# A recurrent state copied out of PSUM in the step that computes it, instead of one step later (gated linear attention inside a transformer block, one core)

## The chip, the cores and the metric

One core of a Trainium2 chip runs the whole block once. The metric is the device time of one execution in microseconds (us), the median of several runs. Engines are named as in the profile: PE is TensorE, DVE is VectorE, ACT is ScalarE, POOL is GpSimd, SP is SyncE (here a queue that issues DMAs).

## What is computed

One transformer block on 1024 tokens of width 1024: a modulated norm, one large input projection, sparse attention over the 256 best keys of each query beside gated linear attention (GLA), an output projection, and a gated feed-forward part. The part around the change is GLA's chunked recurrence:

```
def step(S, inp):
    ...
    o = (jnp.einsum('bhij,bhjv->bhiv', A, vc)
         + jnp.einsum('bhid,bhdv->bhiv', qc * jnp.exp(b), S))
    b_last = b[:, :, -1:, :]
    S = (jnp.exp(b_last)[:, :, 0, :, None] * S
         + jnp.einsum('bhjd,bhjv->bhdv', kc * jnp.exp(b_last - b), vc))
    return S, o
```

Each chunk's output needs the state S that the chunk before it left, and S is the old S, decayed, plus a product over the chunk's keys and values. The kernel uses chunks of 128 tokens (8 of them), and does two heads at a time: `gla0` is heads 0 and 1, `gla1` heads 2 and 3.

## The kernel before, in words

While PE works through the input projections (the *main* job list: groups of 24 or 48 matmuls called units here; lines L243 to L245 and L252 to L254), four *background* jobs advance beside it, a step at a time, at fixed rates per unit: `pump()` (L352) takes each generator in `bg` and calls `next` on it as often as its rate has come due. The four are `ta` and `td` (the search for the 256th largest score, one bit a round, `topk_act` L639 and `topk_dve` L611), and `gla0` and `gla1` (`gla_pair` L773). After each unit, `pin()` (L974) takes the PE and DVE instructions just traced and chains them with dependencies, so **PE and DVE run in exactly the order in which the program text produced them**. ACT, POOL and the DMA queues are not pinned; their order is set by the framework's scheduler.

A round of `ta` is three sign passes on ACT (L654, tiles of 1024, 896 and 768 columns, each with a count) and then four small DVE instructions (L656, L657, L659, L661), the last of which writes the thresholds `Ya` that the next round's passes read. A round of `td` follows on DVE: three counting passes (L625) and L629, L631. The two rounds stand one behind the other in DVE's order.

The end of `gla_pair` is the chunk loop (L882 to L904), nine steps for eight chunks. In step `ch` `chunk(ch)` puts these matmuls on PE, all into one PSUM tile `po` of the tag `pw`, of which there are two buffers: for each head L871 (within the chunk) and, from chunk 1 on, L874 (the carried state, which reads `St`), then L878 for both heads (what the chunk adds to the state). DVE reads that tile twice: L887 or L889 makes the new state `Sn` in SBUF (chunk 0: a copy; later `St` times `el` plus the product), and the pair of L899 adds the two heads' outputs into `gv`, after which ACT squares them (L902, two per chunk). A `pw` buffer is free for the chunk after next when its L899 pair is done.

In the version before, step `ch` begins with the state of chunk `ch - 1`, then issues `chunk(ch)`, then the L899 pair of chunk `ch - 1`:

```
                    Sn = small(P, tag="diag")
                    if ch == 1:
                        V.tensor_copy(Sn, po[:, P:2 * P])
...
            if ch < NT:
                po = chunk(ch)
```

Behind the chunk loop of `gla0` stand, on DVE, more rounds of the search, interleaved with the levels of `gla1`; ACT also casts weights (L219, `whi`) for the next projection there, into a ring of four buffers that PE frees.

Of the kernel before, what the change touches and what calls it, by code (L numbers as in the profile page):

```python
# [15 lines left out]
ALU = mybir.AluOpType  # L16

P = 128
L = 1024
D = 1024  # L20
NT = L // P
# [47 lines left out]
def hymba_block_kernel(  # L69
# [37 lines left out]
    def nm(s):  # L107
        uid[0] += 1
        return f"{s}_{uid[0]}"
# [7 lines left out]
    def ps(shape=(P, 512)):  # L117
        return psp.tile(list(shape), F32, tag="ps", bufs=4, name=nm("ps"))

    def pw(shape=(P, 1024)):  # L120
        return psp.tile(list(shape), F32, tag="pw", bufs=2, name=nm("pw"))

    def small(n=8, dt=F32, tag="sm", bufs=4):
        return sm.tile([P, n], dt, tag=tag, bufs=bufs, name=nm(tag))

    V, A, G, T, S = nc.vector, nc.scalar, nc.gpsimd, nc.tensor, nc.sync
# [261 lines left out]
    def gv_proj(p, w):  # L388
        drain("decay")
        gvt[p] = [g([P, 4, 256]) for _ in range(2)]  # L390
        if p == 0:
            bg["gla0"] = (gla_pair(0, gqk[0, 0], gqk[0, 1], gvt[0], bTs[0]), *RATE["gla0"])
        yield from proj_N_plain(w, gvt[p])
        if p == 0:
            bg["decay"] = (gla_decay(1), *RATE["decay"])
        else:
            drain("gla0")
            bg["gla1"] = (gla_pair(1, gqk[1, 0], gqk[1, 1], gvt[1], bTs[1]), *RATE["gla1"])
# [374 lines left out]
    def gla_pair(p, gq, gk, gv, bT):  # L773
# [48 lines left out]
        el = small(8, tag="el", bufs=2)  # L822
# [40 lines left out]
        St = None  # L863

        def chunk(ch):
            po = pw()
            gvc = gv[ch // 4][:, ch % 4, :]
            for h in range(2):
                hp, dv = slice(64 * h, 64 * h + 64), slice(h * P, (h + 1) * P)
                pd = po[:, h * 512:h * 512 + P]  # L870
                T.matmul(pd, lhsT=AT[ch // 4][:, (ch % 4) * 2 + h, :], rhs=gvc[:, dv],  # L871
                         start=True, stop=(ch == 0))
                if ch > 0:
                    T.matmul(pd, lhsT=gq[hp, ch * P:(ch + 1) * P], rhs=St[hp, :], start=False, stop=True)  # L874
            if ch < NT - 1:
                for h in range(2):
                    hp = slice(64 * h, 64 * h + 64)
                    T.matmul(po[hp, P:2 * P], lhsT=Kn[:, ch, hp], rhs=gvc[:, h * P:(h + 1) * P],  # L878
                             start=True, stop=True)
            return po  # L880

        for ch in range(NT + 1):  # L882
            if ch > 0:
                if ch < NT:
                    Sn = small(P, tag="diag")
                    if ch == 1:
                        V.tensor_copy(Sn, po[:, P:2 * P])  # L887
                    else:
                        V.scalar_tensor_tensor(Sn, St, el[:, ch - 1:ch], po[:, P:2 * P], ALU.mult, ALU.add)  # L889
                    St = Sn  # L890
                done = po
            if ch < NT:
                po = chunk(ch)
            if ch > 0:
                c0 = ch - 1
                gvc = gv[c0 // 4][:, c0 % 4, :]
                for h in range(2):
                    dv = slice(h * P, (h + 1) * P)
                    V.scalar_tensor_tensor(gvc[:, dv], gvc[:, dv], dg[:, 2 * c0 + h:2 * c0 + h + 1],  # L899
                                           done[:, h * 512:h * 512 + P], ALU.mult, ALU.add)  # L900
                    jk = small(P, BF16, tag="jk", bufs=2)
                    A.activation(jk, gvc[:, dv], AF.Square,  # L902
                                 accum_out=ssq_g[:, p, c0 * 2 + h:c0 * 2 + h + 1])
            yield  # L904
# [562 lines left out]
    for n in range(NDG):  # L1467
        ending = n == NDG - 1
        ahead = list(groups[n + 1]) if not ending else []
        for t in range(NT):  # L1470
# [5 lines left out]
            if t % 2:  # L1476
                po = [ps(), ps()]
            else:
                pq = pw()
                po = [pq[:, C0], pq[:, C1]]  # L1480
# [64 lines left out]
```

## Time and profile before

| | |
|---|---|
| three runs, us | 1398.03, 1402.06 (median), 1405.05 |
| the profiled execution, us | 1398.97 |
| its span, first to last instruction | 1397.2 |
| busy: PE, DVE, ACT, POOL | 1308.9, 906.9, 588.3, 413.8 us |
| mean granted TensorE clock | 0.982 of 2.4 GHz |
| chunk loop of gla0 / gla1 on PE | 248.3 to 293.6 us / 397.7 to 442.9 us |

Times inside the kernel are counted from the span's start. A timeline row gives start, duration, engine, line, operation, output and inputs, and in brackets how long the engine had been idle before it and which instruction ended that. Only the profiled execution has such rows; it was 3.09 us quicker than the median.

### The profile page before, as it was taken

What the parts mean: (1) busy time and instruction counts of PE and PEld (TensorE: products, weight loads), DVE (VectorE), ACT (ScalarE), POOL (GpSimd) and SP (SyncE); (2) the same over time, 40 slices, a digit from 0 to 9 for tenths busy, and PEclk for the clock granted to TensorE, in tenths of its full rate; (3) what the DMA queues carried; (4) which work ended last, traced back from release to release, by engine and by line L of the source; (5) the groups of instructions that cost most, each with busy time, mean ns of one, the idle gap of its engine ahead of it and who ended that gap; (6) DMA issues with size and microseconds to landing.
All of it is one profiled execution on the core that took longest, in us unless ns stands there. A gap on an engine that the chain in (4) does not pass through costs nothing.

```text
span 1397.2 us, 18382 instructions
## 1 busy us (share of the span) xinstructions
PE 1308.9 (94%) x6979; PEld 1095.5 (78%) x6979; DVE 906.9 (65%) x1539; ACT 588.3 (42%) x1078; POOL 413.8 (30%) x365
## 2 busy tenths in 40 slices
PE   5899999797799998899998999999999999999997
PEld 3777887696689877798876778878888878888886
DVE  3478899669987756783487666654454556576524
ACT  3367766666562235255673333333232335112202
POOL 3560122122400011213314434444344435222101
PEclk9999999899999999999999999999999999999999
DMA  9701001201120353740322233322222346254102
GB/s 264 216 15 31 16 16 46 76 16 47 60 61 16 121 165 107 271 139 28 121 76 76 91 119 108 121 91 76 91 76 87 125 151 211 95 164 148 46 15 106
DMA packets 93630, 136.36 MB, mean 98 GB/s; under 512 B 6403, under 2 KB 72038, under 8 KB 93542
## 3 DMA queue, kind: packets, MB, share of 16 engines
q1 hardware_dynamic: 89576, 121.49, 27.1%
q0 software_dynamic: 3808, 13.64, 3.1%
q8 instruction: 55, 0.90, 0.3%
q14 instruction: 33, 0.27, 0.1%
q10 hardware_dynamic: 158, 0.06, 0.0%
HBM read 111.04 MB, written 24.13 MB: 97 GB/s over the span
## 4 chain that ended last, share of the span: by engine, by line
PE 63%; DVE 18%; issue 5%; ACT 5%; DMA 3%; POOL 3%; SPq 2%; DVEq 0%; POOLq 0%; ACTq 0%
PE pw L1279 5%; PE pw L1280 4%; PE pw L1281 4%; PE ps L1279 4%; PE ps L1281 4%; PE ps L1280 4%; DVE junk_d L625 3%; PE ps L1486 3%; PE ps L1485 3%; PE ps L1487 3%; PE pw L1486 3%; PE pw L1487 3%; PE pw L1485 3%; ACT junk_a L654 2%; DVE h L798 2%
## 5 line engine op out<-in xcount | busy, mean ns | idle before, releaser
L654 ACT ACTIVATE junk_a<-g,Ya 128x1024 int8<-128x1024 f32 (+2 forms) x96 | 99.9, 1041 | 36.2 <-DVE Ya L661 30.4
L252 PE MATMUL ps<-whi,g 128*128 128x256 f32 x384 | 111.5, 290 | 0.0
L254 PE MATMUL ps<-wlo,g 128*128 128x256 f32 x384 | 109.2, 284 | 0.0
L253 PE MATMUL ps<-whi,g 128*128 128x256 f32 x384 | 109.1, 284 | 0.0
L1310 POOL TENSOR_TENSOR g<-g,h 128x512 f32<-128x512 f32 x33 | 52.2, 1582 | 139.4 <-issue 54.0
L1451 POOL TENSOR_TENSOR raw<-raw,g 128x1024 f32<-128x1024 f32 x22 | 58.2, 2649 | 111.2 <-DMA raw<-in_w_down_dram 101.7
L243 PE MATMUL ps<-g,whi 128*128 128x512 f32 x208 | 83.4, 401 | 0.5 <-DVE dg L853 0.5
L245 PE MATMUL ps<-g,wlo 128*128 128x512 f32 x208 | 81.5, 392 | 1.7 <-DVE wlo L220 1.7
L1281 PE MATMUL ps<-g,wlo 128*128 128x512 f32 x192 | 75.7, 394 | 6.3 <-DVE wlo L1272 6.2
L244 PE MATMUL ps<-g,whi 128*128 128x512 f32 x208 | 81.5, 392 | 0.0
L1279 PE MATMUL pw<-g,whi 128*128 128x512 f32 x192 | 76.9, 401 | 1.5 <-DVE h L1328 1.5
L1279 PE MATMUL ps<-g,wlo 128*128 128x512 f32 x192 | 75.8, 395 | 0.7 <-ACT g L1184 0.7
L252 PEld LDWEIGHTS ps<-whi,g 128*128 128x128 f32 x384 | 74.2, 193 | 2.7 <-issue 2.0
L1280 PE MATMUL ps<-g,wlo 128*128 128x512 f32 x192 | 75.4, 393 | 0.4 <-DVE g L1185 0.4
L1280 PE MATMUL pw<-g,whi 128*128 128x512 f32 x192 | 74.9, 390 | 0.0
L1281 PE MATMUL pw<-g,whi 128*128 128x512 f32 x192 | 74.8, 390 | 0.0
L253 PEld LDWEIGHTS ps<-whi,g 128*128 128x128 f32 x384 | 74.2, 193 | 0.0
L254 PEld LDWEIGHTS ps<-wlo,g 128*128 128x128 f32 x384 | 74.1, 193 | 0.1
L625 DVE TENSOR_SCALAR_CACHE_REDUCE junk_d<-g,Zd 128x640 bf16<-128x640 f32 (+5 forms) x96 | 71.4, 744 | 2.4
L1248 POOL TENSOR_TENSOR gs<-raw,raw 128x512 f32<-128x512 f32 x19 | 25.2, 1325 | 118.8 <-DMA raw<-in_w_gate_up_dram 94.0
L1272 DVE TENSOR_TENSOR whi<-gs,whi 128x512 fp32r<-128x512 f32 x44 | 39.1, 889 | 31.3 <-ACT whi L1271 30.8
L1272 DVE TENSOR_TENSOR wlo<-gs,wlo 128x512 fp32r<-128x512 f32 x44 | 39.1, 889 | 28.8 <-ACT wlo L1271 28.4
(408 smaller groups left out, 3823.0 us busy)
## 6 DMA issues: line engine op xcount, KB each, us to landing
raw<-in_w_gate_up_dram SPq DMA_DIRECT2D x42, 512.0 KB, 3.6
g<-in_w_mod_dram SPq DMA_DIRECT2D x24, 512.0 KB, 8.3
raw<-in_w_in_dram SPq DMA_DIRECT2D x24, 512.0 KB, 4.2
whi<-in_w_mod_dram POOLq DMA_DIRECT2D x24, 512.0 KB, 4.5
hid_d<-g SPq DMA_DIRECT2D x22, 512.0 KB, 3.0
raw<-in_w_down_dram SPq DMA_DIRECT2D x22, 512.0 KB, 4.4
gs<-hid_d SPq DMA_DIRECT2D x22, 512.0 KB, 3.4
g<-in_x_dram SPq DMA_DIRECT2D x16, 512.0 KB, 4.5
```

Source lines behind the costliest of these rows:

```text
L243: T.matmul(pt, lhsT=wh, rhs=rh, start=(k == 0), stop=False)
L252: T.matmul(pt, lhsT=rh, rhs=wh, start=(k == 0), stop=False)
L253: T.matmul(pt, lhsT=rl, rhs=wh, start=False, stop=False)
L254: T.matmul(pt, lhsT=rh, rhs=wl, start=False, stop=(k == KC - 1))
L625: V.tensor_scalar(junk_d[:, :W], top[t] if 0 < i < 16 else score[t], Z[:, j:j + 1].bitcast(F32), -float(TOPK), ALU.is_ge, ALU.add, accum_o ...
L654: A.activation(junk_a[:, :W], score[t], AF.Sign, bias=Y[:, j:j + 1].bitcast(F32), accum_out=acc[:, j:j + 1])
L1279: T.matmul(pt, lhsT=w[:, 0, kk, :], rhs=rh, start=(not more and kk == 0), stop=False, skip_group_check=more)
L1280: T.matmul(pt, lhsT=w[:, 0, kk, :], rhs=rl, start=False, stop=False, skip_group_check=more)
L1281: T.matmul(pt, lhsT=w[:, 1, kk, :], rhs=rh, start=False, stop=(kk == 3), skip_group_check=more)
L1485: T.matmul(po[m], lhsT=ah[:, r], rhs=wh[:, cc], start=(f == 0), stop=False)
L1486: T.matmul(po[m], lhsT=al[:, r], rhs=wh[:, cc], start=False, stop=False)
L1487: T.matmul(po[m], lhsT=ah[:, r], rhs=wl[:, cc], start=False, stop=(f == len(cur) - 1))
```

## The change

The new state of a chunk is made in the same step as the chunk's products, right behind them in the program text; the L899 pair of the chunk before follows it.

```diff
+        po = None
         for ch in range(NT + 1):
-            if ch > 0:
-                if ch < NT:
-                    Sn = small(P, tag="diag")
-                    if ch == 1:
-                        V.tensor_copy(Sn, po[:, P:2 * P])
-                    else:
-                        V.scalar_tensor_tensor(Sn, St, el[:, ch - 1:ch], po[:, P:2 * P], ALU.mult, ALU.add)
-                    St = Sn
-                done = po
+            done = po
             if ch < NT:
                 po = chunk(ch)
+            if ch < NT - 1:
+                Sn = small(P, tag="diag")
+                if ch == 0:
+                    V.tensor_copy(Sn, po[:, P:2 * P])
+                else:
+                    V.scalar_tensor_tensor(Sn, St, el[:, ch:ch + 1], po[:, P:2 * P], ALU.mult, ALU.add)
+                St = Sn
             if ch > 0:
```

The instructions are the same in number and size (L887 becomes L890, L889 becomes L892), and PE's order does not change. DVE's order changes at fourteen instructions, ACT's follows by the scheduler's choice, and on SP one store and one weight load change places in each GLA pair.

DVE, start of gla0's chunk loop. `pw_2354`, `pw_2418` and `pw_2459` are the PSUM tiles of chunks 0, 1 and 2, `diag` the state. Before:

```order
L631 SCALAR_TENSOR_TENSOR Zd<-md_2325,Zd 128x3
L656 TENSOR_TENSOR acca_2359<-acca_2359,need 128x3
...
L631 SCALAR_TENSOR_TENSOR Zd<-md_2372,Zd 128x3
L217 CAST whi_2378<-raw_2376 128x1024
L217 CAST whi_2384<-raw_2382 128x1024
L887 COPY diag_2416<-pw_2354 128x128
L899 SCALAR_TENSOR_TENSOR g_1531<-g_1531,dg_1589,pw_2354 128x128 x2
L889 SCALAR_TENSOR_TENSOR diag_2457<-diag_2416,el_1590,pw_2418 128x128
L899 SCALAR_TENSOR_TENSOR g_1531<-g_1531,dg_1589,pw_2418 128x128 x2
```

The same place with the change:

```order
L631 SCALAR_TENSOR_TENSOR Zd<-md_2325,Zd 128x3
L890 COPY diag_2359<-pw_2354 128x128
L656 TENSOR_TENSOR acca_2361<-acca_2361,need 128x3
...
L631 SCALAR_TENSOR_TENSOR Zd<-md_2374,Zd 128x3
L217 CAST whi_2380<-raw_2378 128x1024
L217 CAST whi_2386<-raw_2384 128x1024
L892 SCALAR_TENSOR_TENSOR diag_2425<-diag_2359,el_1590,pw_2418 128x128
L899 SCALAR_TENSOR_TENSOR g_1531<-g_1531,dg_1589,pw_2354 128x128 x2
L892 SCALAR_TENSOR_TENSOR diag_2466<-diag_2425,el_1590,pw_2459 128x128
L899 SCALAR_TENSOR_TENSOR g_1531<-g_1531,dg_1589,pw_2418 128x128 x2
```

The copy of chunk 0's state has moved ahead of one round of the search and two casts; the state of chunk 1 has taken the place that the copy had, ahead of chunk 0's L899 pair. The start of gla1's loop moves in the same way (there one round lies between).

ACT, end of gla0's chunk loop. `acca_2755` is the first round of the search behind the loop, `jk` the squares of the last two chunks, `whi_2773` the cast of the next weights. Before:

```order
L654 ACTIVATE junk_a,acca_2755<-g_796,Ya 128x1024
L654 ACTIVATE junk_a,acca_2755<-g_797,Ya 128x896
L347 COPY g_2389<-ps_2627 128x256
L654 ACTIVATE junk_a,acca_2755<-g_798,Ya 128x768
L902 ACTIVATE jk_2718,ssq_g<-g_1532 128x128
L902 ACTIVATE jk_2721,ssq_g<-g_1532 128x128
L347 COPY g_2389<-ps_2684 128x256
L902 ACTIVATE jk_2750,ssq_g<-g_1532 128x128
L902 ACTIVATE jk_2753,ssq_g<-g_1532 128x128
L654 ACTIVATE junk_a,acca_2805<-g_796,Ya 128x1024
L219 CAST whi_2773<-raw_2771 128x1024
```

The same place with the change:

```order
L654 ACTIVATE junk_a,acca_2755<-g_796,Ya 128x1024
L654 ACTIVATE junk_a,acca_2755<-g_797,Ya 128x896
L347 COPY g_2391<-ps_2686 128x256
L902 ACTIVATE jk_2718,ssq_g<-g_1532 128x128
L902 ACTIVATE jk_2721,ssq_g<-g_1532 128x128
L902 ACTIVATE jk_2750,ssq_g<-g_1532 128x128
L902 ACTIVATE jk_2753,ssq_g<-g_1532 128x128
L219 CAST whi_2773<-raw_2771 128x1024
L654 ACTIVATE junk_a,acca_2755<-g_798,Ya 128x768
```

The round's third sign pass has moved behind the four squares of the last two chunks and behind the weight cast.

DVE, in gla1's loop, around the end of the search. `pw_3861` and `pw_3944` are the tiles of chunks 3 and 4. Before, the state of chunk 3 stands there, and with the change that of chunk 4; the first fence is before, the second with the change:

```order
L633 TENSOR_TENSOR Zd<-md_3887,Zd 128x3
L889 SCALAR_TENSOR_TENSOR diag_3942<-diag_3859,el_2920,pw_3861 128x128
L899 SCALAR_TENSOR_TENSOR g_2388<-g_2388,dg_2919,pw_3861 128x128 x2
L666 TENSOR_SCALAR Ya<-Ya 128x3
L667 TENSOR_SCALAR Fa<-Fa 128x3
```

```order
L633 TENSOR_TENSOR Zd<-md_3889,Zd 128x3
L892 SCALAR_TENSOR_TENSOR diag_3951<-diag_3868,el_2920,pw_3944 128x128
L899 SCALAR_TENSOR_TENSOR g_2390<-g_2390,dg_2919,pw_3861 128x128 x2
L666 TENSOR_SCALAR Ya<-Ya 128x3
L667 TENSOR_SCALAR Fa<-Fa 128x3
```

What moved there is that the final selection of the search (from L666 on) now stands behind a read of chunk 4's products.

## Rows read from the trace of the kernel before

**Rows 1.** Page, part 4: shares of the chain that ended last, by engine.

```profile
PE 63%; DVE 18%; issue 5%; ACT 5%; DMA 3%; POOL 3%; SPq 2%; DVEq 0%; POOLq 0%; ACTq 0%
```

**Rows 2.** Timeline of PE, gla0, chunks 0 to 3.

```profile
249.01 0.44 PE L878 MATMUL pw<-g,g 128*64 128x128 f32 x4
...
260.43 0.77 PE L874 MATMUL pw<-diag,g 64*128 64x128 f32 x2 [7.50 <-DVE diag L887]
...
267.42 0.39 PE L871 MATMUL pw<-g,g 128*128 128x128 f32 x2
267.74 0.48 PE L874 MATMUL pw<-diag,g 64*128 64x128 f32 x2
...
272.34 0.39 PE L871 MATMUL pw<-g,g 128*128 128x128 f32 x2
```

**Rows 3.** Timeline of DVE, the same stretch.

```profile
254.35 0.16 DVE L631 SCALAR_TENSOR_TENSOR Zd<-md,Zd 128x3 int32<-128x3 int32 x1
255.47 0.16 DVE L656 TENSOR_TENSOR acca<-acca,need 128x3 f32<-128x3 f32 x1 [0.96 <-ACT junk_a L654]
...
258.79 1.29 DVE L217 CAST whi<-raw 128x1024 fp32r<-128x1024 f32 x2
260.00 0.28 DVE L887 COPY diag<-pw 128x128 f32<-128x128 f32 x1
...
263.32 0.35 DVE L889 SCALAR_TENSOR_TENSOR diag<-diag,el,pw 128x128 f32<-128x128 f32 x1 [2.52 <-PE pw L878]
```

**Rows 4.** Stretches: us, busy (count) of PE, PEld, DVE, ACT, POOL, clock, DMA, GB/s.

```profile
257.00:259.00 2.00, 0.00 (x0) 0.00 (x0) 1.86 (x9) 1.94 (x5) 0.00 (x0) 0.50 0.00 0
...
404.40:406.30 1.90, 0.03 (x1) 0.00 (x0) 1.79 (x8) 1.87 (x5) 0.00 (x0) 1.00 0.00 0
...
300.00:350.00 50.00, 41.41 (x288) 38.71 (x287) 43.67 (x109) 32.52 (x55) 11.41 (x8) 0.93 0.16 49
```

**Rows 5.** Timeline at the end of gla0's loop: PE, ACT, DVE, POOL in turn.

```profile
294.85 0.28 PE L253 MATMUL ps<-whi,g 128*128 128x256 f32 x1
...
294.10 0.31 ACT L902 ACTIVATE jk<-g 128x128 bf16<-128x128 f32 x1 [1.54 <-DVE g L899]
...
296.12 1.03 ACT L219 CAST whi<-raw 128x1024 fp32r<-128x1024 f32 x1
...
298.49 0.94 ACT L654 ACTIVATE junk_a<-g,Ya 128x768 int8<-128x768 f32 x1
...
293.66 0.60 DVE L899 SCALAR_TENSOR_TENSOR g<-g,dg,pw 128x128 f32<-128x128 f32 x2 [3.67 <-PE pw L874]
294.19 0.15 DVE L656 TENSOR_TENSOR acca<-acca,need 128x3 f32<-128x3 f32 x1
...
299.55 0.16 DVE L656 TENSOR_TENSOR acca<-acca,need 128x3 f32<-128x3 f32 x1 [0.80 <-ACT junk_a L654]
299.75 1.73 DVE L657 TENSOR_SCALAR ma<-acca 128x3 int32<-128x3 int32 x1
...
299.61 1.84 POOL L777 MEMSET g<- 128x1024 f32 x2
```

**Rows 6.** Timeline in gla1's loop: PE, then DVE.

```profile
404.05 0.38 PE L871 MATMUL pw<-g,g 128*128 128x128 f32 x2
406.38 0.48 PE L874 MATMUL pw<-diag,g 64*128 64x128 f32 x2 [1.95 <-DVE diag L887]
...
425.25 0.44 PE L878 MATMUL pw<-g,g 128*64 128x128 f32 x4
...
402.72 0.16 DVE L656 TENSOR_TENSOR acca<-acca,need 128x3 f32<-128x3 f32 x1 [1.08 <-ACT junk_a L654]
...
419.06 0.34 DVE L889 SCALAR_TENSOR_TENSOR diag<-diag,el,pw 128x128 f32<-128x128 f32 x1
...
438.44 0.35 DVE L889 SCALAR_TENSOR_TENSOR diag<-diag,el,pw 128x128 f32<-128x128 f32 x1 [6.51 <-PE pw L878]
```

**Rows 7.** Groups by line and form, 246 to 450 us: busy, mean ns | idle before.

```profile
L657 DVE TENSOR_SCALAR ma<-acca 128x3 int32<-128x3 int32 x21 | 7.3, 346 | 0.8
```

## Prediction

> **What bounds the kernel now.** I read the shares of the ending chain first: PE holds 63% of it and DVE 18% [rows 1], so a stall of PE is usually worth its length, and in some stretches DVE is what PE waits for. The change touches two chunk loops, so I went to the timeline of PE there, to see which matmuls had idle time before them. There are two such stalls. In gla0, chunk 1's first L874 waits 7.50 us for the state copy L887 [rows 2]; in gla1 the same matmul waits 1.95 us [rows 6]. Then I read DVE's timeline, to see why the copy was late. It was not the data: chunk 0's products ended at 249.45 (249.01 + 0.44) [rows 2]. DVE reached L887 only at 260.00, because a round of the search (from 255.47) and two weight casts (258.79) stood ahead of it in the fixed order [rows 3]. Last I read how the loop ends. DVE takes up the last L899 pair at 293.66, after waiting 3.67 us for PE; from there the engines change roles: the next rounds go back and forth between DVE and ACT (DVE waits 0.80 us for a sign pass at 299.55) [rows 5], until PE is waiting for DVE again at 406.38 [rows 6]. So gla0's loop is bound by PE, the 110 us behind it by DVE and ACT together, and gla1's loop by PE again.
>
> **What the change removes, gla0.** In the new order the copy stands right behind the L631 that started at 254.35 and took 0.16 [rows 3], so it starts at 254.51. PE followed the copy's start by 0.43 (260.00 to 260.43) [rows 2, 3], so chunk 1's L874 starts at 254.94 instead of 260.43. The copy's 0.28 us lie in the 0.96 us for which DVE waited on ACT anyway before 255.47 [rows 3], so they cost nothing; if ACT were earlier, they would cost 0.28.
>
> The clock matters next. After the 7.50 us stall PE stood at a granted clock of 0.50, that is 1.2 GHz [rows 4], and went from chunk 1's L874 to chunk 2's L871 in 6.99 us (260.43 to 267.42), where chunk 2 to chunk 3 took 4.60 (267.74 to 272.34) [rows 2]. The new stall is some 2.0 us long (7.50 - 5.49). The nearest row is gla1's stall of 1.95 us [rows 6], during which the clock stayed at 1.00, 2.4 GHz [rows 4]. I therefore take 4.60: PE reaches chunk 2 at 259.54.
>
> There a new wait appears. Chunk 2 writes into the PSUM buffer of chunk 0, which is free only after chunk 0's L899 pair. In the new order this pair follows chunk 1's state, and that takes the place the copy had, at 260.00, behind the casts. With 0.35 for the state [rows 3] and 0.60 for the pair [rows 5], the buffer is free at 260.95 and chunk 2 starts at about 261.0. Against 267.42 that is 6.4 us earlier. If the clock fell after all, PE would arrive at 261.93 (254.94 + 6.99), 0.9 later.
>
> From chunk 2 on, PE needs 4.92 us per chunk (267.42 to 272.34) [rows 2], and DVE makes each state as soon as the products end, long before PE wants it. The sign rounds that stand between two states take DVE less than the 9.8 us of two chunks. So PE keeps its 6.4 us to the end of the loop, and the last L899 pair starts at about 287.3.
>
> **What comes back: ACT's order.** DVE could take up its next round 6.4 us earlier, but that round's third sign pass is now queued on ACT behind the squares of the last two chunks and behind the cast L219. The squares follow the pair by 0.44 (293.66 to 294.10) [rows 5] and end, with their reads, some 0.9 us after that, at about 288.7. The cast needs a weight buffer that PE frees with the L253 that ended at 295.13 (294.85 + 0.28) [rows 5]; 6.4 earlier is 288.7 as well. It takes 1.03, and the third pass takes 1.06 until DVE moves (298.49 to 299.55) [rows 5]. DVE's L656 then starts at 290.8 instead of 294.19: 3.4 us, not 6.4. One round later part of this returns, since the cast no longer lies in that round: before, from L656 to L656 took 5.36 (294.19 to 299.55) with 0.80 of waiting for ACT; without the cast ACT needs 4.33 and DVE 4.56, so the next L656 starts at 295.36 instead of 299.55, a gain of 4.2.
>
> The L657 behind it took 1.73 us; it ran beside two memsets on POOL that ended at 301.45 (299.61 + 1.84), just when L657 did [rows 5]. POOL reaches these memsets by a chain that starts with the last squares, 7.8 us before their end (293.66 to 301.45), so they would now run from about 293.3 to 295.1, before that L657. Its 1.56 us of delay would go, and with it the gain grows to 5.8. But the round before then has its small instructions at 293.9, inside the memsets, and if those are held until 295.1 that costs 1.2. I take 4.6, because L629 there is the same kind of instruction as the L657 that was held; the bounds are 4.2 (the whole delay comes back) and 5.8 (none does). [...]
>
> **gla1.** The new copy stands before the round that starts at 402.72 after a wait of 1.08 [rows 6], so its 0.28 us are hidden again. An L874 follows its chunk's L871 by 0.32 (267.42 to 267.74) [rows 2]; chunk 1's L871 was at 404.05 [rows 6], so its L874 starts at 404.37 instead of 406.38: **2.0 us**. A new wait lies behind it: chunk 4's state is now read before the final selection. DVE would be there at about 420.1 (419.06 plus the two instructions and the pair moved ahead, 1 us), while chunk 4's products end at 423.7 (425.25 + 0.44 - 2.0) [rows 6]; so the final selection starts some 4.6 us later against DVE's old times. It is covered by the 6.51 us for which DVE waited before 438.44 [rows 6]; without that cover it would cost 2.6 (4.6 less the 2.0 that PE gained).
>
> On SP the store of a parked projection now goes ahead of one weight load in each loop; its data are ready before that load's buffer is free, so I count nothing; the price if not is the store's issue, under 1 us. Fourteen instructions keep their sizes: nothing there.
>
> **Sum.** 4.6 + 2.0 = 6.6 us; own bounds 5.3 (4.2 + 2.0 - 0.9) to 7.8 (5.8 + 2.0). The profiled execution would take 1398.97 - 6.6 = 1392.4; it lay 3.1 below the median of 1402.06, so the median becomes **1395.5**. A measurement of this kernel can tell about 0.5%, 7.0 us: the forecast lies just inside.
>
> **Rivals.**
> *ACT's queue does not hold the round back* (the cast finds its buffer free earlier, or ACT is ahead of DVE). Then PE's 6.4 us go through whole, with the 1.56 of the L657: 6.4 + 1.6 + 2.0 = 10.0, 1392.1. For it speaks that DVE waited only 0.80 for ACT at 299.55 [rows 5]; against it that the cast and the pass are in sequence in the new order.
>
> *Only gla1's stall pays.* The DVE and ACT stretch from 294 to 404 gives the first gain back, as a weight load or a level of gla1 is late by itself: 2.0 us, 1400.1. Against it: all waits I saw there are of DVE, ACT and PE for one another, which move together.
>
> *The small DVE instructions meet POOL more often* (the slower end). L657 alone cost 21 x (0.346 - 0.17) = 3.7 us by such delays [rows 7]. POOL runs eight instructions between 300 and 350 [rows 4], and the new phase could lay each over a round. One meeting costs 1.56; from the fifth more than before (6.6 / 1.56 = 4.2) the kernel is slower; with all eight and as many in the 50 us behind, 16 x 1.56 - 6.6 = 18.4, up to 1420.5. [...]
>
> *No effect.* The copy is earlier, but rounds between DVE and ACT were the true limit already inside gla0's loop: 1402.1. Against it: DVE waited 2.52 and 3.67 us for PE there [rows 3, 5].
>
> **Chances.** Forecast 0.50 (own range 1393.5 to 1397.5; 0.20 of it beyond 0.5%), ACT's queue harmless 0.20 (all faster), only gla1 0.18 (0.01 faster, 0.16 same, 0.01 slower, by the scatter of the runs), POOL 0.06 (0.04 slower, 0.02 same), no effect 0.06 (same). Together: faster 0.41, same 0.54, slower 0.05. The range goes from 1390.0 (the first rival, less 2 for the scatter of three runs over 7 us) to 1401.0 (the second, plus 1); outside lie POOL, no effect, and the tails of the rest, about 0.2.
>
> **What would show it.** In the new profile: chunk 1's L874 in gla0 at about 254.9 after an idle time near 2, with the clock at 2.4 GHz; chunk 2's L871 near 261.0 after a short wait for L899; the last pair near 287.3; the following L656 near 290.8 after an idle time ended by L654; in gla1 no wait before chunk 1's L874, and one of some 3.6 us on DVE before chunk 4's state. The forecast is wrong if that L656 starts before 289 or after 293, or if the distance from it to gla1's chunk 1 is longer than before by over 2 us.

## The result, and the profile after

The changed kernel takes 1393.78 us (median of 6 runs, 1392.31 to 1396.39) against 1400.92 us for the kernel before on the same chip (6 runs): a ratio of 0.9944 with a 95% interval of 0.9927 to 0.996, so about 7.1 us faster. Measured once more beside its variants it took 1392.63 us, a ratio of 0.9928 (0.9909 to 0.9946). The profiled execution went from 1398.97 to 1392.39 us, its span from 1397.2 to 1390.7.

The shares of the ending chain in the changed kernel, part 4 of the page, answer to [rows 1]:

```profile
PE 68%; DVE 18%; issue 5%; ACT 4%; DMA 3%; POOL 2%; DVEq 0%; ACTq 0%; POOLq 0%
```

PE's share has grown by 5 points, from 63% to 68%, and DVE's has stayed. In the changed file the copy of chunk 0's state is L890 and the later states are L892. All times in this region lie 0.08 us later than before (gla0's first L871 at 248.56 instead of 248.48).

The timeline of PE in gla0's loop, in the changed kernel, against [rows 2]:

```profile
248.56 0.60 PE L871 MATMUL pw<-g,g 128*128 128x128 f32 x4
252.63 0.39 PE L871 MATMUL pw<-g,g 128*128 128x128 f32 x2
254.94 0.46 PE L874 MATMUL pw<-diag,g 64*128 64x128 f32 x2 [1.92 <-DVE diag L890]
...
261.07 0.46 PE L871 MATMUL pw<-g,g 128*128 128x128 f32 x2
...
266.05 0.39 PE L871 MATMUL pw<-g,g 128*128 128x128 f32 x2
```

The wait before chunk 1's L874 is 1.92 us instead of 7.50, and chunk 2 starts at 261.07 instead of 267.42. There is no idle time before chunk 2. The stretches of the same time (us, busy time of PE, PEld, DVE, ACT and POOL, granted clock, DMA share, GB/s) say why:

```profile
255.00:257.00 2.00, 2.00 (x12) 1.47 (x13) 1.36 (x5) 2.00 (x5) 0.00 (x0) 0.87 0.00 2
257.00:259.00 2.00, 2.00 (x11) 2.00 (x11) 1.86 (x9) 1.97 (x6) 0.00 (x0) 0.50 0.65 262
259.00:261.00 2.00, 2.00 (x15) 1.91 (x13) 1.92 (x5) 1.29 (x5) 1.32 (x1) 0.78 0.00 0
```

The clock did fall to 0.50 after the shorter stall. PE worked through 255 to 261 without a gap, at half clock for part of it: at 0.50 its 128x256 matmuls started every 0.213 us (L254 at 257.12 to L252 at 259.25), and at 1.00 every 0.119 us (L253 at 260.01 to L254 at 260.84). The rows give the granted clock as a share of full speed; 1.2 GHz for 0.50, and with it 2.4 GHz for 1.00, is no more than an estimate from the first of these paces (256 columns in 0.213 us, 1.20 columns a ns), and the second falls short of it (2.15 columns a ns).

The timeline of DVE at both ends of the same loop, in the changed kernel, against [rows 3, 5]:

```profile
254.50 0.28 DVE L890 COPY diag<-pw 128x128 f32<-128x128 f32 x1
255.54 0.16 DVE L656 TENSOR_TENSOR acca<-acca,need 128x3 f32<-128x3 f32 x1 [0.75 <-ACT junk_a L654]
...
260.32 0.60 DVE L899 SCALAR_TENSOR_TENSOR g<-g,dg,pw 128x128 f32<-128x128 f32 x2
...
286.94 1.12 DVE L899 SCALAR_TENSOR_TENSOR g<-g,dg,pw 128x128 f32<-128x128 f32 x4
290.89 0.16 DVE L656 TENSOR_TENSOR acca<-acca,need 128x3 f32<-128x3 f32 x1 [2.83 <-ACT junk_a L654]
...
293.93 0.80 DVE L629 TENSOR_SCALAR md<-acc 128x3 int32<-128x3 f32 x1
...
295.99 0.15 DVE L656 TENSOR_TENSOR acca<-acca,need 128x3 f32<-128x3 f32 x1
296.18 0.17 DVE L657 TENSOR_SCALAR ma<-acca 128x3 int32<-128x3 int32 x1
```

Of the 6.3 us that PE gained, 2.83 become a wait of DVE for the sign pass on ACT. One round later the L657 that took 1.73 takes 0.17, and the L629 before it takes 0.80 instead of the 0.17 that it has in rounds with POOL idle.

The same end of the loop on ACT, and then on POOL:

```profile
288.88 1.05 ACT L219 CAST whi<-raw 128x1024 fp32r<-128x1024 f32 x1 [0.28 <-PE ps L253]
289.83 0.93 ACT L654 ACTIVATE junk_a<-g,Ya 128x768 int8<-128x768 f32 x1
...
292.86 1.85 POOL L777 MEMSET g<- 128x1024 f32 x2
```

And gla1's loop, PE and then DVE, against [rows 6]:

```profile
393.43 0.60 PE L871 MATMUL pw<-g,g 128*128 128x128 f32 x4
399.95 0.38 PE L871 MATMUL pw<-g,g 128*128 128x128 f32 x2
400.26 0.48 PE L874 MATMUL pw<-diag,g 64*128 64x128 f32 x2
...
394.45 0.29 DVE L890 COPY diag<-pw 128x128 f32<-128x128 f32 x1 [0.72 <-PE pw L878]
419.61 0.35 DVE L892 SCALAR_TENSOR_TENSOR diag<-diag,el,pw 128x128 f32<-128x128 f32 x1 [3.61 <-PE pw L878]
```

Chunk 1's L874 has no wait, and DVE waits 3.61 us before chunk 4's state.

### The profile page after: what moved, and what is told of

Its sections match the earlier page's. It is cut to its first block, busy times and chain, and to the rows that moved or that the text cites. A ratio compares the mean times of both kernels' runs of the same rounds, so it can differ in the third digit from the quotient of the medians.

```text
span 1390.7 us, 18382 instructions
## 1 busy us (share of the span) xinstructions
PE 1315.2 (95%) x6979; PEld 1101.8 (79%) x6979; DVE 908.6 (65%) x1539; ACT 588.1 (42%) x1078; POOL 413.6 (30%) x365
## 4 chain that ended last, share of the span: by engine, by line
PE 68%; DVE 18%; issue 5%; ACT 4%; DMA 3%; POOL 2%; DVEq 0%; ACTq 0%; POOLq 0%
PE pw L1279 5%; PE pw L1280 4%; PE pw L1281 4%; PE ps L1279 4%; PE ps L1281 4%; PE ps L1280 4%; PE pw L1485 3%; PE pw L1486 3%; PE ps L1485 3%; PE ps L1486 3%; PE pw L1487 3%; DVE junk_d L625 3%; PE ps L1487 3%; PE ps L252 2%; PE ps L253 2%
## 5 line engine op out<-in xcount | busy, mean ns | idle before, releaser
L654 ACT ACTIVATE junk_a<-g,Ya 128x1024 int8<-128x1024 f32 (+2 forms) x96 | 99.9, 1041 | 32.4 <-DVE Ya L661 26.6
L252 PE MATMUL ps<-whi,g 128*128 128x256 f32 x384 | 112.3, 293 | 0.0
L253 PE MATMUL ps<-whi,g 128*128 128x256 f32 x384 | 109.9, 286 | 0.0
L254 PE MATMUL ps<-wlo,g 128*128 128x256 f32 x384 | 109.9, 286 | 0.0
L252 PEld LDWEIGHTS ps<-whi,g 128*128 128x128 f32 x384 | 75.1, 196 | 2.5 <-issue 1.9
L254 PEld LDWEIGHTS ps<-wlo,g 128*128 128x128 f32 x384 | 74.9, 195 | 0.1
L253 PEld LDWEIGHTS ps<-whi,g 128*128 128x128 f32 x384 | 75.0, 195 | 0.0
L625 DVE TENSOR_SCALAR_CACHE_REDUCE junk_d<-g,Zd 128x640 bf16<-128x640 f32 (+5 forms) x96 | 71.4, 744 | 2.4
```

What stands on the lines that cost most here:

```text
L252: T.matmul(pt, lhsT=rh, rhs=wh, start=(k == 0), stop=False)
L253: T.matmul(pt, lhsT=rl, rhs=wh, start=False, stop=False)
L254: T.matmul(pt, lhsT=rh, rhs=wl, start=False, stop=(k == KC - 1))
L625: V.tensor_scalar(junk_d[:, :W], top[t] if 0 < i < 16 else score[t], Z[:, j:j + 1].bitcast(F32), -float(TOPK), ALU.is_ge, ALU.add, accum_o ...
L654: A.activation(junk_a[:, :W], score[t], AF.Sign, bias=Y[:, j:j + 1].bitcast(F32), accum_out=acc[:, j:j + 1])
```

## The experiments

One distance serves as the measure of both loops in what follows: from gla0's first L871 to the first L871 of gla1's chunk 7. It was 192.82 us before (248.48 to 441.30) and 186.62 in the changed kernel (248.56 to 435.18). What is left behind chunk 7 took 954.8 to 959.6 us over all profiled executions, whichever kernel it was, so one execution's time cannot tell the small edits apart, and the distance can.

| kernel | median, us | ratio to before (95%) | distance, us |
|---|---|---|---|
| changed | 1393.78 | 0.9944 (0.9927 to 0.996) | 186.62 |
| changed, again (e7) | 1392.63 | 0.9928 (0.9909 to 0.9946) | 185.56 |
| gla0 alone (e1) | 1395.06 | 0.9954 (0.9939 to 0.9968) | 186.39 |
| gla0 alone, again (e12) | 1395.09 | 0.9959 (0.9942 to 0.9975) | 186.54 |
| gla1 alone (e2) | 1399.63 | 0.9984 (0.9972 to 0.9995) | 190.85 |
| matmuls in the stall (e3) | 1394.34 | 0.9947 (0.9931 to 0.9963) | 187.13 |
| third pass first (e4) | 1392.32 | 0.9932 (0.9918 to 0.9946) | 186.32 |
| both (e5) | 1394.67 | 0.9938 (0.9918 to 0.9959) | 186.84 |
| and products ahead of casts (e6) | 1392.55 | 0.9925 (0.9905 to 0.9944) | 183.81 |
| the same, again (e11) | 1392.56 | 0.9939 (0.9927 to 0.9952) | 184.05 |
| matmuls before the last L809 (e8) | 1398.12 | 0.9968 (0.9954 to 0.9983) | 190.82 |
| the same, own PSUM tile (e9) | 1394.87 | 0.996 (0.9948 to 0.9973) | 186.32 |
| e6 with e9 (e10) | 1392.56 | 0.9944 (0.993 to 0.9957) | 183.89 |

**The two loops apart (e1, e2, e12).** The state is made at the new place for one pair and at the old place for the other:

```diff
+        early = p == 0
...
         for ch in range(NT + 1):
             done = po
+            if not early and 0 < ch < NT:
+                St = state(ch - 1)
             if ch < NT:
                 po = chunk(ch)
-            if ch < NT - 1:
+            if early and ch < NT - 1:
...
```

In e2 the first line reads p == 1. Expected of gla0 alone:

> The new place of the copy in the first pair's loop alone; the second pair's loop as before. Theory (each pair pays by itself, the first one most): chunk 1's L874 matmul of the first pair at about 254.9 us, the DVE rounds about 5.1 us earlier from 296 us on, and in the second pair the wait of 1.95 us before chunk 1's L874 is back, so 4.2 to 5.2 us faster than the kernel before (about 1396.2). Rival (only the second pair pays, the first pair's gain is lost in the selection rounds): within 0.7 us of the kernel before.

Expected of gla1 alone:

> The new place of the copy in the second pair's loop alone; the first pair's loop as before. Theory: the wait of 1.95 us before chunk 1's L874 of the second pair is gone and nothing else moves up to there, so 2.0 us faster than the kernel before (about 1398.9). Rival (the second pair carries the whole gain): 6 to 7 us faster. If this and the run with the first pair alone add up to the change's 7 us, the two loops don't interact.

gla0 alone gave 5.65 us (1400.71 to 1395.06; 4.2 to 5.2 expected), gla1 alone 1.1 us (2.0 expected), with a distance shorter by 1.97 (192.82 to 190.85), so both loops can pay by themselves, and the rival "only gla1" is out. The two medians' gains add up to 6.7 us, near the 7.1 of the whole change. But the distance of gla0 alone (186.39) is already that of the whole change's first execution (186.62), since the wait that I expected back in gla1 did not come back. PE, then DVE, in gla1's loop of gla0 alone (in this file L888 is the copy, at its old place):

```profile
399.50 0.48 PE L874 MATMUL pw<-diag,g 64*128 64x128 f32 x2
...
397.46 0.28 DVE L888 COPY diag<-pw 128x128 f32<-128x128 f32 x1
```

DVE reaches the old place at 397.46, and at 406.04 in the kernel before. That is 8.6 us earlier; 0.45 of it is the start of this execution (gla0's first L871 at 248.03), and gla0's loop explains 5.2. The rest, some 2.8, comes from the round that begins at 390.93 in the kernel before; two of its small instructions met two operations on POOL (the second pair of rows is POOL's):

```profile
390.93 0.88 DVE L656 TENSOR_TENSOR acca<-acca,need 128x3 f32<-128x3 f32 x1 [0.99 <-ACT junk_a L654]
392.05 2.27 DVE L659 COPY_PREDICATED Fa<-ma,Ya 128x3 int32<-128x3 int32 x1
...
390.76 1.05 POOL L215 TENSOR_SCALAR whi<-raw 128x1024 fp32r<-128x1024 f32 x1 [15.29 <-PE ps L253]
391.89 2.40 POOL L220 TENSOR_TENSOR wlo<-raw,whi 128x1024 fp32r<-128x1024 f32 x1
```

L656 takes 0.16 and L659 0.17 where POOL is idle. With gla0's rounds shifted, the same two POOL operations meet one L629 instead, which takes 1.26 us in e1, and that delay costs DVE nothing: the next L656 starts without the wait of 1.08 us for ACT that it has in the kernel before. So DVE got further ahead than PE, and the copy at its old place was in time by 1.6 us (397.46, and the 0.43 by which PE follows it, against 399.50).

This depends on the execution. In the changed kernel's second execution (e7, below) the round met both POOL operations again: L656 took 0.80 us at 386.09, and L659 2.27. DVE, then PE, in that execution:

```profile
387.13 2.27 DVE L659 COPY_PREDICATED Fa<-ma,Ya 128x3 int32<-128x3 int32 x1
...
401.05 0.16 DVE L631 SCALAR_TENSOR_TENSOR Zd<-md,Zd 128x3 int32<-128x3 int32 x1
...
399.44 0.48 PE L874 MATMUL pw<-diag,g 64*128 64x128 f32 x2
```

The copy's old place is behind that L631, at 401.13. From there chunk 1's L874 would have started at 401.56, 2.1 us later than it did (an estimate from these rows and the 0.43). So in that execution the new place in gla1 was worth 2 us beside gla0's gain, and in the first execution it was worth nothing (398.14 + 0.43 against 400.26). Worked out in the same way, the old place would have been late in two of the twelve profiled executions that have gla0's new place (e7, and e3 by 1.9 us), and in time by 0.6 us or more in the ten others. By the trace the two gains are 6.4 us (e1) and 2.0 us (e2) alone, and 6.2 and 7.3 together (the changed kernel's two executions): they add up in the second and not in the first.

The times of gla0 alone did not fit a second gain of nothing, so it was measured again:

> The first pair alone once more, to settle whether the second pair's new place adds anything. If it adds nothing (the trace of the first run shows chunk 1's L874 of the second pair without a wait, since DVE reaches the old place of the copy 8.6 us earlier): 6.5 to 8 us faster than the kernel before, like the changed kernel. If it adds its 2.0 us: 4.5 to 5.7 us faster.

It gave 1395.09, 5.6 us, which is what was expected if gla1's new place adds its 2.0 us, though its trace again has no wait in gla1's loop (distance 186.54; the copy was in time by 0.6 us). Over 11 runs each, gla0 alone has a mean of 1395.1 us and the changed kernel of 1393.2. Of these 2 us, 0.35 lie outside the span: the time exceeds it by 2.0 to 2.2 us in every run of e1, e2 and e12, and by 1.6 to 1.9 in every run of the other kernels. Where the rest is was not found. Some runs of gla0 alone may have had the wait in gla1, as an execution like e7's would; behind the loops PE and DVE have the same order in both kernels, but ACT's order differs in gla1's loop, and SP's at one place there (a store and a weight load), and behind the loops the profiled executions of one kernel differ by about as much. So the times say that gla1's new place still adds something, and the profiled executions of gla0 alone don't show it.

**The clock in the shortened stall (e3).** Four matmuls into columns of the chunk's PSUM tile that nobody reads:

```diff
                 T.matmul(pd, lhsT=AT[ch // 4][:, (ch % 4) * 2 + h, :], rhs=gvc[:, dv],
                          start=True, stop=(ch == 0))
+                if p == 0 and ch == 1 and h == 0:
+                    for _ in range(FILL):
+                        T.matmul(po[:, 768:896], lhsT=AT[0][:, 2, :], rhs=gvc[:, 0:P], start=True, stop=True)
```

> The changed kernel, with four more matmuls of 128x128 (f32, into unused columns of the chunk's PSUM tile, read by nobody) between chunk 1's first L871 and its first L874 in the first pair, where TensorE was idle for 1.92 us. Theory (two limits meet at 261.1 us: the low clock that follows the idle time, and the L899 pair that frees chunk 2's PSUM buffer): the clock stays at 2.4 GHz from 255 to 260 us, chunk 2's L871 then waits about 1.4 us for DVE's L899 and starts at 261.1 as before, and the time is that of the changed kernel within 0.4 us. Rival (the low clock alone holds chunk 2): chunk 2's L871 at about 259.6 and 1.4 us faster than the changed kernel. Second rival (the fillers make chunk 1's L874 late): it starts after 255.3 and the time is longer by what it is late.

PE in that kernel, and the stretches behind (L872 and L878 are the matmuls that are L871 and L874 in the changed kernel, L876 the added ones, L903 the L899):

```profile
252.38 0.39 PE L872 MATMUL pw<-g,g 128*128 128x128 f32 x2
252.61 1.06 PE L876 MATMUL pw<-g,g 128*128 128x128 f32 x8
254.70 0.46 PE L878 MATMUL pw<-diag,g 64*128 64x128 f32 x2 [1.03 <-DVE diag L894]
...
260.83 0.46 PE L872 MATMUL pw<-g,g 128*128 128x128 f32 x2 [1.41 <-DVE g L903]
...
267.26 0.39 PE L872 MATMUL pw<-g,g 128*128 128x128 f32 x2
```

```profile
255.00:257.00 2.00, 2.00 (x16) 1.51 (x15) 1.57 (x7) 2.00 (x5) 0.00 (x0) 1.00 0.00 1
...
263.00:265.00 2.00, 2.00 (x11) 1.91 (x10) 1.69 (x8) 0.69 (x4) 1.43 (x1) 0.50 0.85 232
```

The clock stays at 1.00 from 255 to 261 us, and the predicted wait of 1.4 us (1.41) for the L899 pair appears: chunk 2 starts 8.45 us after chunk 1's first product, in the changed kernel 8.44. Two limits do meet there. What I had not expected is the second half: the clock falls to 0.50 after the new wait (263 to 265 us), and chunk 3 comes 14.88 us after chunk 1 (252.38 to 267.26), in the changed kernel 13.42 (252.63 to 266.05). The low clock was put off and not avoided. The time, 0.6 us above the changed kernel's, is within what its runs scatter.

**ACT's order (e4).** The squares of chunks 6 and 7 are traced behind the third sign pass, and the cast is put behind it too (`behind` adds an order without a semaphore):

```diff
+                    if p == 0 and c0 >= 6:
+                        late.append(square)
...
+            if len(late) == 4:
+                for square in late:
+                    behind(square(), done)
+                late.clear()
+                cast_behind.append(done)
...
-                A.copy(hi, raw)
+                i = A.copy(hi, raw)
+                if cast_behind:
+                    behind(i, cast_behind.pop())
```

> The changed kernel, with ACT's order changed at one place: the third sign pass L654 of the selection round that follows the first pair's last chunk stands ahead of the four squares of chunks 6 and 7 and of the weight cast L219, instead of behind them. Theory (ACT's order gave back about 2.7 us there): the third pass starts at 287.1 instead of 289.8 us, DVE's L656 at 288.2 instead of 290.9; the squares and the cast then stand ahead of the next round's first pass, which starts 0.3 to 1.4 us earlier than now, so the next L656 comes 0.5 to 1.5 us earlier than 295.99 and the time is 0.3 to 1.5 us under the changed kernel's. Rival (ACT's order costs nothing, DVE or PE would have waited anyway): within 0.3 us of the changed kernel, though the third pass is early. Second rival (the memsets on POOL meet the next round's L657 again): no gain or up to 1 us slower.

DVE's timeline there (L912 and L669 are L899 and L656 of the changed kernel):

```profile
288.41 1.11 DVE L912 SCALAR_TENSOR_TENSOR g<-g,dg,pw 128x128 f32<-128x128 f32 x4
289.51 0.16 DVE L669 TENSOR_TENSOR acca<-acca,need 128x3 f32<-128x3 f32 x1
...
296.13 0.16 DVE L669 TENSOR_TENSOR acca<-acca,need 128x3 f32<-128x3 f32 x1 [1.84 <-ACT junk_a L662]
```

The wait of 2.83 us is gone: L669 follows 1.10 us after the last L912 group's start, in the changed kernel 3.95 (286.94 to 290.89). The next round is held by ACT (1.84), as the squares and the cast still have to run, so of the 2.85 us 1.33 stay (7.72 from group to second L656, in the changed kernel 9.05), as expected. So the order on ACT did hold that round, by 2.85 us where the prediction had 3.0 (6.4 less 3.4). In this execution the clock was at 0.50 until about 262.7 instead of 259.9, and chunk 3 came 14.74 us after chunk 1 instead of 13.42. That ate the 1.3 us, and the distance is shorter by 0.3 only. The median of 1392.32 is below both measurements of the changed kernel, by 1.5 and 0.3 us, which the intervals don't separate.

**What holds chunk 2 (e5, e6, e11).** e5 has the edits of e4 and seven matmuls instead of four. e6 also puts the state and the L899 pair of chunk 1's step ahead of the two casts L217 in DVE's fixed order:

```diff
+            at = len(nc.cur_bb.bb.instructions)
...
+            if p == 0 and ch == 1:
+                front.update(i.name for i in nc.cur_bb.bb.instructions[at:] if i.engine == mybir.EngineType.DVE)
             yield
...
+        new.sort(key=lambda i: i.name not in front)
```

> The changed kernel with both: seven such f32 matmuls before chunk 1's first L874 of the first pair (four left 1.03 us idle), and the third sign pass ahead of the squares and the cast. Theory (the clock's low stretch costs nothing where it ends before the L899 pair frees the buffer, but 1.3 us where it lasts longer, as in the profiled run of the kernel with the early pass): chunk 2's L871 8.45 us after chunk 1's first L871, as in the changed kernel, the early pass gives 1.3 us, and the time is 1 to 2 us under the changed kernel's, about 1392.3. Rival (the early pass gives nothing): within 0.5 us of the changed kernel.

> The run before this one, and on DVE the state and the L899 pair of the first pair's step of chunk 1 stand ahead of the two casts L217 of 0.6 us each instead of behind them. Theory (with the clock high, the L899 pair is what holds chunk 2): the pair ends 1.2 us earlier, chunk 2's L871 comes 7.2 us after chunk 1's first L871 instead of 8.45, and the time is another 1.0 to 1.3 us down, about 1391. Rival (what is won there is eaten by ACT's queue at the end of the loop, where the selection round waits): chunk 2 early, time unchanged within 0.4 us.

In e5 chunk 2 came 8.45 us after chunk 1 and chunk 3 14.92, as in e3: the clock fell behind the new wait again (0.50 from 265 to 267 us), which the theory had left out. The distance is no shorter, and the time, 1394.67 where about 1392.3 was expected, is not under the changed kernel's. PE and the clock in e6 (L885 and L891 for L871 and L874, L917 for L899):

```profile
253.75 0.39 PE L885 MATMUL pw<-g,g 128*128 128x128 f32 x2
...
256.06 0.46 PE L891 MATMUL pw<-diag,g 64*128 64x128 f32 x2 [0.36 <-DVE diag L908]
...
261.00 0.46 PE L885 MATMUL pw<-g,g 128*128 128x128 f32 x2 [0.21 <-DVE g L917]
...
265.97 0.39 PE L885 MATMUL pw<-g,g 128*128 128x128 f32 x2
```

```profile
257.00:259.00 2.00, 2.00 (x17) 1.71 (x18) 1.90 (x7) 1.97 (x5) 0.00 (x0) 1.00 0.28 113
```

Chunk 2 comes 7.25 us after chunk 1 (7.2 expected), the clock stays at 1.00 (255 to 265 us), and chunk 3 comes after 12.22. Both limits are removed at once, and the distance, 183.81, is 2.8 and 1.8 us shorter than in the changed kernel's two executions (186.62 and 185.56). It was run again:

> The kernel with the first three edits once more, beside the two others: 8 to 10 us faster than the kernel before, and chunk 2's L871 again 7.25 us after chunk 1's first L871 with the clock at 2.4 GHz.

The distance was 184.05. The times, 1392.55 and 1392.56, don't show it clearly: over 11 runs each the mean is 1392.0 us, and 1393.2 for the changed kernel, with runs of one kernel 3 to 6 us apart. By the trace this is the best version of the study; by the times it is no slower than the change, and whether it is faster stays open.

**The changed kernel again (e7).**

> The changed kernel as it is, once more, beside its variants on one chip: 6 to 8 us faster than the kernel before; the clock low for 3 to 7 us after the wait before chunk 1's L874.

It was 8.6 us faster than before (6 to 8 expected). Its distance is 1.06 shorter than in the first execution of the same program. The difference lies at one place, the last L809 group of gla1. First the stretches of the first execution there, then those of the second:

```profile
366.00:368.00 2.00, 2.00 (x11) 2.00 (x11) 1.97 (x2) 0.73 (x1) 2.00 (x2) 0.50 0.00 0
368.00:370.00 2.00, 2.00 (x15) 2.00 (x14) 2.00 (x1) 0.00 (x0) 2.00 (x1) 0.72 0.00 0
```

```profile
366.00:368.00 2.00, 2.00 (x16) 2.00 (x15) 2.00 (x2) 1.06 (x1) 2.00 (x1) 0.79 0.00 0
368.00:370.00 2.00, 2.00 (x19) 2.00 (x19) 1.97 (x2) 0.00 (x0) 2.00 (x2) 1.00 0.00 0
```

After much the same idle time (5.81 and 5.86 us) L809 starts at 363.65 and 364.03. The low clock (0.50) lasts to about 369.1 in one and to 366.8 in the other, and the next group, L850, follows after 10.15 and 8.95 us.

**Matmuls before that group (e8, e9, e10).** e8 puts nineteen matmuls into the tile that L809 is about to fill; e9 eighteen into a tile of their own:

```diff
             pts[lv] = pt
+            spare = ps() if p == 1 and lv == 6 else None
+            for _ in range(WARM if spare is not None else 0):
+                T.matmul(spare[:, 0:P], lhsT=ident, rhs=ident, start=True, stop=True)
```

> The changed kernel, with nineteen f32 matmuls of 128x128 (their product is overwritten) ahead of the last L809 group of the second pair, where TensorE is idle for 5.81 us and then works 5.8 us at 1.2 GHz. Theory (1.1 us of what the first pair's loop gives is lost between that group and the second pair's loop, because the low clock there lies on work for 5.8 us instead of 2.7 us in the kernel before): L809 starts when it did, the clock stays at 2.4 GHz, the next group L850 follows after 7.3 us instead of 10.15, the second pair's loop begins 2.5 to 3 us earlier, and the time is 1.5 to 3 us under the changed kernel's. Rival (DVE's selection rounds set the end, so the low clock there costs nothing): the time of the changed kernel within 0.5 us, with TensorE waiting for DVE in the second pair's loop. ACT's order of two sign passes and a copy moves with this edit, which can cost some tenths.

> The changed kernel, with eighteen f32 matmuls of 128x128 into a PSUM tile of their own ahead of the last L809 group of the second pair; nothing reads the tile, and it needs no buffer that DVE still holds. Theory (the low clock after that wait costs 0.5 us where it is short, 2.9 us where it is long): L809 starts when it did, the next group L850 follows after 7.3 us (10.15 and 8.9 in the two profiled runs of the changed kernel), and the time is 0.5 to 2.5 us under the changed kernel's. Rival (DVE or ACT set the start of the second pair's loop): the time of the changed kernel within 0.5 us. Some copies of PSUM on ACT move behind sign passes with this edit, which can cost some tenths.

> All that helped together: seven matmuls before chunk 1's L874, the step's products ahead of the casts on DVE, the third sign pass early, and the eighteen matmuls ahead of the last L809 group. If each pays by itself: chunk 2 7.25 us after chunk 1's first L871, L850 7.3 us after L809, and 2 to 4 us under the changed kernel's time, about 1390. Rival (DVE's rounds take over between the two loops): the time of the kernel with the first three edits, within 0.5 us.

e8 was a miss of mine, 4 to 6 us slower than the changed kernel where 1.5 to 3 us faster was expected: the tile's buffer was still held by DVE's masked copy two levels back. The added matmuls and L812 (the L809 of that file) on PE:

```profile
363.63 6.46 PE L810 MATMUL pw<-ident 128*128 128x128 f32 x38 [6.60 <-DVE g L821]
369.92 1.95 PE L812 MATMUL pw<-h,gs 128*128 128x128 f32 x16
```

They waited for DVE until 363.63 and then stood 6.3 us ahead of L812. It answers another question: a delay of that group passes on to the end. Counted from gla0's first L871, L812 starts 6.8 us later than L809 in the changed kernel (121.89 and 115.09); the group behind it follows after 7.54 us instead of 10.15, as L812's sixteen matmuls took 1.95 us and those of L809 3.75, which gives 2.6 back; and the distance grows by the 4.2 that are left, the median by 4.3 (against e7, measured beside it, by 5.3 and 5.5). In e9 they ran in the idle time as meant. PE in e9:

```profile
364.14 2.02 PE L813 MATMUL pw<-h,gs 128*128 128x128 f32 x16 [1.79 <-DVE h L799]
371.75 1.84 PE L854 MATMUL ps<-hsel,gs 128*128 128x2 f32 x16
...
380.74 0.39 PE L253 MATMUL ps<-whi,g 128*128 128x256 f32 x1 [0.42 <-ACT g L348]
385.30 0.39 PE L253 MATMUL ps<-whi,g 128*128 128x256 f32 x1 [1.42 <-DVE dg L857]
```

The sixteen matmuls took 2.02 us, and the next group follows after 7.61 us, as expected, but PE then waits 0.42 us for ACT and 1.42 for DVE, and the distance is 186.32, in the changed kernel 186.62 and 185.56. The time, 1394.87, is not under the changed kernel's either. e10 has the distance of e6 and the time of e11 (1392.56), where about 1390 was the forecast. So the rivals hold as far as the distance goes: what the faster group gives there (7.61 us to the next instead of 10.15), DVE and ACT take back. How much of that is due to the copies on ACT that moved with the edit was not separated.

## Why the prediction was right

The time came out as forecast: 6.6 us predicted, 6.6 in the profiled execution (1398.97 to 1392.39), about 7.1 by the medians. The forecast of 1395.5 for the median started from 1402.06 in three runs; over six runs the kernel before has 1400.92, and the changed one 1393.78. That the profiled executions agree to the tenth is luck: gla0's term came out 0.5 above the 4.6, 0.9 was lost again between the loops, and runs of one kernel lie 3 to 6 us apart. Neither sign of being wrong came: the L656 behind the loop started at 290.89, and from it to gla1's chunk 1 there are 109.06 us, before 109.86. By its steps:

- **The copy's place: right.** L890 at 254.50 (predicted 254.51), L874 at 254.94 (254.94), DVE's wait for ACT behind it 0.75 instead of 0.96: the copy was free.
- **The clock: wrong, and harmless.** "The nearest row is gla1's stall of 1.95 us [rows 6], during which the clock stayed at 1.00 ... I therefore take 4.60" failed. The row covers the idle time alone, and in the changed kernel the clock fell to 0.50 1.5 us after PE had begun again, behind an idle time of 1.92 us. PE reached chunk 2 at 261.07 without waiting, not at 259.54 with a short wait behind it. It cost nothing, because the L899 pair ended at 260.92 (260.32 + 0.60) anyway. The forecast "chunk 2 near 261.0" was thus met for half the reason; e3 showed the other half, and e6, which removes both, starts chunk 2 1.2 us sooner. That it was harmless is partly luck: in five of the seven profiled executions with this stall chunk 2 came 8.44 to 8.46 us after chunk 1, and in two (e4 and e8) the low clock lasted longer and cost 1.3 (9.74 and 9.76).
- **ACT's queue: right.** L656 at 290.89 (290.8) after a wait for L654; e4 took the wait away. The rival "ACT's queue harmless" is out.
- **The memsets: right in kind, half the size.** L629 was held, but 0.63 us (0.80 less 0.17) instead of 1.2: the memsets ended at 294.71, not 295.1, and the 1.2 had the instruction's own 0.17 in it. With it the term is 4.2 + 1.56 - 0.63 = 5.13, and the trace has 5.13 at the round's end (L661 at 296.58, before 301.71). The passes L625 beside the same memsets kept their times (0.75 and 0.61). In the kernel before, the L656 and L659 at 390.93 and 392.05 were held as well (0.88 and 2.27 us, with POOL idle 0.16 and 0.17): they ended at 391.81 and 394.32, beside POOL's L215 and L220, which ended at 391.81 and 394.29. That L629 would be held as L657 had been was an assumption, and it came true; what decides which instruction of DVE is held was not shown.
- **Between the loops: not foreseen.** The 5.1 us are 4.2 at gla1's chunk 0 in the first execution (149.05 us from gla0's first L871 before, 144.87 after), and 5.2 in the second (143.81). The difference is the length of the low clock at one L809.
- **gla1: the size right, the term not independent.** Without the wait, 2.0 us, as e2 has it. But the sum treated it as a second gain beside gla0's in any case. e1 and e12 show that gla0's gain alone can remove that wait, as DVE gains more than PE (8.6 us in e1); the rows of e7 show an execution in which it would not have, where the new place was worth 2.1. So the 2.0 us are a second gain in some executions and none in others. The medians lie nearer to adding up (5.6 and 1.1 us alone, 7.1 and 8.6 together), and how often the wait would be there is open. The new wait before chunk 4's state, 3.61 us, was there and cost nothing (predicted 3.6).
- **POOL.** The meetings were re-dealt. In the first execution this was in the kernel's favour: the two at 390.93 and 392.05 (0.72 and 2.10 us too long) became one. In the second execution of the same program both were back (0.80 and 2.27 us), so the dealing is a matter of the execution. A rival that counts only new meetings, as mine did, leans to the slow side.

Of the rivals, "only gla1" is refuted by e1, "no effect" by the result.

## What to carry to other kernels

When an early stall is shortened, look at each later stall again with the new times before adding up: a wait that was a matter of lag on another engine may go by itself, and by a margin of a microsecond it may do so in one execution and not in the next. Where a stall gets short but does not vanish, give two starts for what follows, one at each clock level (here 0.50 and 1.00), and see whether another limit (here the PSUM buffer) lies behind both; if it does, the clock's price is nothing as long as the low stretch ends before that limit, and keeping the clock high gains nothing until that limit is moved too (e3 and e5; moving that limit alone was not run). And price a changed position on a third engine's queue by its order, not by its busy time: ACT was busy 42% of the span and held DVE for 2.8 us.

## What was not expected of the hardware

In these traces the granted clock does not follow from the length of an idle time alone. PE's idle of 1.95 us in gla1 of the kernel before left it at 1.00, during it [rows 4, 6] and in the work behind it:

```profile
406.30:412.00 5.70, 5.62 (x40) 4.85 (x40) 5.46 (x15) 2.83 (x12) 0.00 (x0) 1.00 0.33 76
```

The 1.92 us in gla0 of the changed kernel, 1.41 us in e3 (after 1.03 us some 5 us earlier) and 1.41 us in e5 (after 0.36) were followed by 0.50; 0.36 and 0.21 us in e6 were not (1.00 from 255 to 265 us). After these short waits the clock fell 0.8 us (e4) to 2.5 us (e5) after work had begun again, and after the same wait of 1.92 us it was low until about 259.9 in the changed kernel and until about 262.7 in e4, which is the same program up to there. This is worth 1.3 us in gla0's loop, and 1.1 us at the last L809 between one program's two executions (distances of 186.62 and 185.56). Such stretches behind the loops (954.8 to 959.6 us for work that is the same) may make most of what runs of this kernel differ by: that part is argued from the profiles, and not tested.
